# Sums of weights for a feed-forward layer on one Trainium2 core: smaller transfers and no pacing copies

## The chip, the core and the metric

The kernel runs on one core of one Trainium2 chip. A core has a matrix engine (TensorE; PE in the profile, with PEld for its weight loads), VectorE (DVE), ScalarE (ACT), GpSimd (POOL) and SyncE (SP), each with its own queue of instructions, and 16 DMA engines that all queues share. The metric is the device time of one execution in microseconds (us), and the median of several runs. A profile of one execution goes with it; times within it count from the start of its span.

## The reference, cut to what matters

One decoder layer on 512 tokens of width 1024 in float32: half a step of a gated feed-forward, an attention mixer with two branches, half a step of a second feed-forward, a last normalisation. The change touches the first feed-forward only.

```python
def _swiglu(x, w_gate, w_up, w_down):
    return (jax.nn.silu(x @ w_gate) * (x @ w_up)) @ w_down
...
h = h + FFN_HALF * _swiglu(_rmsnorm(h, norm_ffn1[i]), ffn1_gate[i], ffn1_up[i], ffn1_down[i])
```

`ffn1_gate` and `ffn1_up` are 1024 x 2816, `ffn1_down` is 2816 x 1024.

## The kernel before

**Numbers in two parts.** Every matrix product is made of three: each float32 operand is split into a high part that TensorE takes exactly and a low part, and high x high, high x low and low x high are added in PSUM. Weights come from DRAM as blocks of 512 KB (`raw`, four buffers, loaded by SP, line 137). ScalarE casts the high part (`whi`, line 145), VectorE subtracts for the low part (`wlo`, line 149), TensorE multiplies (`mm`, line 379, or line 747 in the units below). Blocks are split two ahead of their use. A block of the first feed-forward feeds 24 matmuls of 512 columns.

**The first feed-forward** (`ffn`, line 772) goes over 22 column tiles of 128 (f-tiles) in thirds: 0 to 7, 8 to 15, 16 to 21. After each third its part of `ffn1_down` is multiplied, in eight blocks, and added to `h` (line 821). In the first third, sums and differences of the activations are also made (`sums_of_u`), which the second third needs.

**The second third** is computed with seven half-size products instead of eight (`unit`, line 718), two f-tiles a unit, four units in all. Four of the seven multiply sums and differences of quarters of `ffn1_gate` and `ffn1_up`: s1 = u0 + u1, s3 = g0 + u0, s2 = s1 + g0, s4 = s2 + g1, where g0, g1, u0, u1 are the upper and lower halves of the two matrices in these columns. DMA makes these sums from DRAM to DRAM: GpSimd issues a plain copy (line 440) or an adding transfer (line 438) for each step of `unit_sums` (line 429). Each step that reads what an earlier one wrote waits for it in GpSimd's queue, and everything behind it in that queue waits too. SP loads the finished sums like other weights (`raw<-s`).

**The order of the sums.** `CHUNK` (line 32) says how many f-tiles one set of sums covers: 4, so there are two sets ("chunks") of 8 steps, each step a transfer of 512 rows of 2 KB. `adds` is the generator of these steps. Two steps are issued after the first f-tile that the loop computes (f == 3 at that place). Each further step goes through `pace` (line 713): GpSimd first copies one column of something just computed (`G`, or `h` in the down product), so that the step can't be issued before that exists. After the loops what is left of the steps is issued.

**What else stands in GpSimd's queue** at that time: the masks of the attention (`build_masks`, lines 538 to 552), issued from `side_work` (line 927) after the fourth f-tile; the last of them clears `fold`. One f-tile later VectorE writes into `fold` (lines 931 and 932) and so waits for GpSimd. Later `rope_tables` (line 554) has ScalarE issue two loads of 31 integers each into `pc` (line 562), one integer to a partition, and VectorE reads `pc` at line 565, between the low parts of the down blocks.

Of the kernel before, what the change touches and what calls it, by code (L numbers as in the profile page):

```python
# [8 lines left out]
F32 = mybir.dt.float32  # L9
# [19 lines left out]
NEVER = 1e9  # L29
STEPS = (1, 0), (5, 0), (2, 0), (1, 1), (5, 1), (2, 1), (6, 0), (6, 1), (3, 0), (3, 1), (4, 0), (4, 1), (7, 0), (7, 1)  # L30
PRODUCTS = 1, 6, 5, 2, 7, 3, 4
CHUNK = 4
LAST_ROWS = 0, 1, 4, 5, 2, 3
LAST_ORDER = 0, 1, 4, 5, 2, 3
TOP = 3e38
# [23 lines left out]
def f32(ap):  # L59
    return ap.bitcast(F32)  # L60


class Weights:
# [110 lines left out]
    def next(self):  # L174
        i = self.pos
        self.prep(i + self.AHEAD)
        self.pos += 1
        return self.place(i)
# [178 lines left out]
def layer(ctx, tc, a, out):  # L357
    nc = tc.nc
    tensor, scalar, vector, gpsimd = nc.tensor, nc.scalar, nc.vector, nc.gpsimd
    const = ctx.enter_context(tc.tile_pool(name="const", bufs=1))  # L360
# [7 lines left out]
    def acc(filler=True):  # L368
        turn[0] += 1
        return psum.tile([128, 512], F32, name="acc" if filler else ("acc", "o", "s")[turn[0] % 3])  # L370
# [48 lines left out]
    def chunks(tiles):  # L419
        return [(f, min(CHUNK, tiles[1] - f)) for f in range(tiles[0], tiles[1], CHUNK)]  # L420

# [3 lines left out]
    def sum_tile(n, f, k):  # L425
        t, i = s_sums[n, f, k]
        return t if i == 0 else s_sums[n, t, k][0]

    def unit_sums(n):


        for f, nf in chunks(UNITS[n]):
            g0, g1, u0, u1 = (half(n, what, kh, f, nf) for what in ("gate", "up") for kh in range(2))
            s1, s2, s3, s4 = (sum_tile(n, f, k) for k in range(1, 5))
            for o, i, add in ((s1, u0, 0), (s3, g0, 0), (s1, u1, 1), (s3, u0, 1), (s2, s1, 0), (s2, g0, 1), (s4, s2, 0),
                              (s4, g1, 1)):
                if add:
                    gpsimd.dma_start(o, i, accum_op=OP.add)
                else:
                    gpsimd.dma_start(o, i)  # L440
                yield

    def unit_block(n, f, m):
# [4 lines left out]
        k = {5: 1, 6: 2, 7: 3, 3: 4}[m]  # L448
        c = (f - UNITS[n][0]) % CHUNK * 128
        return sum_tile(n, f, k).rearrange("(k p) c -> p k c", p=128)[:, :, c:c + 256]  # L450
# [59 lines left out]
    G = main.tile([128, 16, S], F32R, name="G")  # L510
# [122 lines left out]
    def col_of(sums):  # L633
        v = temp.tile([128, 4], F32, name="nv", bufs=1)
        vector.tensor_scalar(v, sums, 1.0 / D, EPS, op0=OP.mult, op1=OP.add)
        y = temp.tile([128, 4], F32, name="ny", bufs=1)
        gpsimd.tensor_tensor(y, v, mhalf, op=OP.pow)
        b = temp.tile([128, 4], F32, name="nb", bufs=1)
        vector.tensor_tensor(b, y, y, op=OP.mult)
        vector.tensor_tensor(b, b, v, op=OP.mult)  # L640
        vector.tensor_scalar(b, b, -0.5, 1.5, op0=OP.mult, op1=OP.add)
        col = temp.tile([128, 4], F32, name="rcol", bufs=1)
        vector.tensor_tensor(col, y, b, op=OP.mult)
        return col

    def norm_rows(col):
        dg = sqacc.rearrange("p (t c) -> p t c", t=4)
        for t in range(4):
            vector.tensor_scalar(dg[:, t], ident, col[:, t:t + 1], None, op0=OP.mult)
        ps = tbank()  # L650
        for t in range(4):
            mm(ps[:, t], ones, dg[:, t], True, True)
        scalar.copy(r_b, flat(ps))


    def mm3(ps, w, x, n, amid=None):
        (wh, wl), (xh, xl) = w, x
        for k in range(n):
            if amid is not None and k == n * 3 // 4:
                amid()  # L660
            mm(ps, wh[:, k], xh(k), k == 0, False)
            mm(ps, wh[:, k], xl(k), False, False)
            mm(ps, wl[:, k], xh(k), False, k == n - 1)
# [4 lines left out]
    def swiglu(pg, pu, j):  # L668
        z = temp.tile([128, S], F32, name="z")
        vector.tensor_tensor(z, pg, r_b, op=OP.mult)  # L670
        s = temp.tile([128, S], F32, name="s")
        scalar.activation(s, z, AF.Silu)
        t = temp.tile([128, S], F32, name="t")
        vector.tensor_tensor(t, pu, r_b, op=OP.mult)
        g = temp.tile([128, S], F32, name="g")
        vector.tensor_tensor(g, s, t, op=OP.mult)
        split(G[:, j], G[:, 8 + j], g)
# [3 lines left out]
    def sums_of_u(n, k):  # L681


        g1, g2 = gains[:, n, k:k + 1], gains[:, n, 4 + k:5 + k]
        (h11, h12), (h21, h22) = ((h[:, d, :256], h[:, d, 256:]) for d in (k, 4 + k))
        b, p, q = (temp.tile([128, 2, 256], F32, name=name) for name in "zst")
        scalar.activation(b[:, 0], h12, AF.Identity, scale=g1)
        scalar.activation(b[:, 1], h22, AF.Identity, scale=g2)
        vector.scalar_tensor_tensor(p[:, 0], h11, g1, b[:, 0], op0=OP.mult, op1=OP.subtract)
        vector.tensor_tensor(p[:, 1], b[:, 1], p[:, 0], op=OP.add)  # L690
        vector.tensor_tensor(q[:, 0], b[:, 0], b[:, 1], op=OP.subtract)
        vector.scalar_tensor_tensor(q[:, 1], h21, g2, p[:, 1], op0=OP.mult, op1=OP.subtract)
        for i, x in ((0, p), (2, q)):
            split(both["hi"][:, k, i:i + 2], both["lo"][:, k, i:i + 2], x)
# [11 lines left out]
    def settle(todo):  # L706
        for x in todo:
            x()
        todo.clear()

    pace_t = const.tile([128, 1], F32, name="pace")

    def pace(adds, after):

        gpsimd.tensor_copy(pace_t, after)
        next(adds, None)

    def unit(j):


# [51 lines left out]
    def ffn(after, begun, side, sums, early):  # L772


        norm = {}

        def col():
            norm["col"] = col_of(sums)

        def rows():  # L780
            norm_rows(norm["col"])
            for j, b in enumerate(begun):
                swiglu(*b, j)

        lo, hi = UNITS[1]
        adds = unit_sums(1)
        for third, (f0, f1) in enumerate(THIRDS):
            f = f0 + (len(begun) if f0 == 0 else 0)
            while f < f1:
                if lo <= f < hi:  # L790
                    unit(f - f0)
                    f += 2
                    if f > lo + 2:
                        next(early, None)
                    continue
                first = f == len(begun)
                pg = acc(False)
                mm3(pg, W.next(), u_in, KD, col if first else None)
                pu = acc(False)
                mm3(pu, W.next(), u_in, KD, rows if first else None)  # L800
                swiglu(pg, pu, f - f0)
                f += 1
                if third == 0:
                    if f > 4:
                        sums_of_u(0, f - 5)
                    if f == 3:
                        next(adds)
                        next(adds)
                    for j in (8 + f - 1, f - 1) if f < 7 else (f - 1,):
                        pace(adds, f32(G[:, j, :1]))  # L810
                else:
                    next(early, None)
                next(side, None)
            settle(later)
            settle(owed)
            for d in range(KD):
                po = acc(False)
                mm3(po, W.next(), g_in, f1 - f0)
                if third == 2 and d < KD - 1:
                    W.prep(W.pos + W.AHEAD)  # L820
                vector.scalar_tensor_tensor(h[:, d], po, 0.5, h[:, d], op0=OP.mult, op1=OP.add)
                if third == 0:
                    next(side, None)
                    if d < 4:
                        pace(adds, h[:, d, :1])
                if third == 1 and d in (0, 2, 4, 6, 7):
                    next(early, None)
                if third == 2:
                    after(d)
        for g in (adds, side, early):  # L830
            for _ in g:
                pass
# [4 lines left out]
    with pool("h1") as h_pool, pool("temp1", 2) as temp, pool("tables") as tables, ExitStack() as starting:  # L837
        start = starting.enter_context(pool("start"))
        h = h_pool.tile([128, KD, S], F32, name="h")
# [107 lines left out]
        with pool("stage", 2) as stage, pool("both") as sums_pool:  # L947
            both["hi"], both["lo"] = (sums_pool.tile([128, 4, 4, 256], F32R, name=n) for n in ("bhi", "blo"))
            ffn(to_mix, begun, side_work(), sums=sums0, early=W.early(stage))
# [3 lines left out]
    with ExitStack() as mixing:  # L953
# [703 lines left out]
        h = h_pool.tile([128, KD, S], F32, name="h")  # L1657
# [247 lines left out]
```

## Time and profile before

| What | Before |
|---|---|
| median of 3 runs | 1129.09 us (1125.06 to 1131.6) |
| the profiled execution, its own time | 1128.45 us |
| its span | 1126.7 us |
| mean granted clock of TensorE | 0.994 |
| bytes moved by DMA | 186.28 MB, mean 165 GB/s |
| q0 (transfers that GpSimd issues) | 10880 packets, 33.56 MB, 12.8% of 16 engines |
| q1 (transfers that SP issues) | 190536 packets, 147.38 MB, 43.2% of 16 engines |
| first issue of a sum, last issue of a sum | 35.16 us, 142.09 us |

The profiled execution is one of many; its span runs from the first to the last instruction, and its own time is 1.75 us longer. The first third of the feed-forward with its down product reaches to about 153 us, the four units from there to about 231 us. Rows of the chain and of an engine's instructions begin with their start and length in microseconds; in brackets stands how long the engine had been idle and what ended that. Rows of waits give the total, the times and the longest.

### The profile page before, as it was taken

The numbers are of one execution on the slowest core, as the hardware profiler recorded it, in microseconds if no ns is written. First come the engines' busy times: TensorE is split into PE (matmuls) and PEld (weight loads), VectorE is DVE, ScalarE is ACT, GpSimd is POOL, SyncE is SP. The second block draws the span as 40 slices with busy tenths as digits, with TensorE's granted clock in tenths as the row PEclk, the third lists the DMA queues.
The fourth block names the chain that finished last, engine by engine and source line by source line (L and its number), as shares of the span: only waits on it lengthen the run. The fifth ranks groups of instructions, "written<-read, shape, count | busy, mean of one in ns | idle before, by whom it ended". The sixth has DMA issues, their size and how long they took to land.

```text
span 1126.7 us, 15645 instructions
## 1 busy us (share of the span) xinstructions
PE 1104.6 (98%) x5859; PEld 946.4 (84%) x5859; DVE 714.4 (63%) x1299; ACT 495.7 (44%) x922; POOL 184.0 (16%) x219
## 2 busy tenths in 40 slices
PE   9999899999999999999999999999999999999997
PEld 8878699988888999989888888888888888888876
DVE  5667468874566569887777646654567754685553
ACT  5435134542334446766667643433334332342332
POOL 0122000000001235654333422120000000000002
PEclk9999899999999999999999999999999999999999
DMA  7499966698766446737667455633234633354212
GB/s 230 150 250 266 250 179 195 203 297 267 225 205 196 130 121 172 187 118 179 203 163 235 117 178 165 177 94 112 76 99 144 191 89 113 103 176 132 83 68 75
DMA packets 204164, 186.28 MB, mean 165 GB/s; under 512 B 6772, under 2 KB 175544, under 8 KB 203960
## 3 DMA queue, kind: packets, MB, share of 16 engines
q1 hardware_dynamic: 190536, 147.38, 43.2%
q0 software_dynamic: 10880, 33.56, 12.8%
q10 hardware_dynamic: 2672, 4.35, 1.0%
q8 instruction: 46, 0.75, 0.3%
q14 instruction: 30, 0.25, 0.1%
HBM read 165.34 MB, written 53.48 MB: 194 GB/s over the span
## 4 chain that ended last, share of the span: by engine, by line
PE 89%; DVE 4%; issue 2%; DMA 2%; ACT 2%; POOL 1%; POOLq 0%; ACTq 0%; DVEq 0%; SPq 0%
PE acc L379 32%; PE s L379 23%; PE o L379 23%; PE o L747 3%; PE tp L1596 2%; PE s L747 2%; PE acc L747 2%; DMA pc<-in_positions_dram 1%; DVE wlo L149 1%; ACT whi L145 1%; DMA raw<-in_cmp_k_w_dram 1%; PE tp L379 1%; DVE turn_a L1294 0%; PE tp L885 0%; PE tp L1222 0%
## 5 line engine op out<-in xcount | busy, mean ns | idle before, releaser
L149 DVE TENSOR_TENSOR wlo<-raw,whi 128x1024 fp32r<-128x1024 f32 (+2 forms) x201 | 229.9, 1166 | 44.7 <-ACT whi L145 44.4
L145 ACT CAST whi<-raw 128x1024 fp32r<-128x1024 f32 (+2 forms) x226 | 203.0, 925 | 110.0 <-PE acc L379 30.5
L379 PE MATMUL acc<-uh,whi 128*128 128x512 f32 x296 | 117.9, 398 | 0.0
L379 PE MATMUL acc<-uh,wlo 128*128 128x512 f32 x296 | 115.8, 391 | 0.0
L379 PE MATMUL acc<-ul,whi 128*128 128x512 f32 x296 | 115.6, 390 | 0.0
L379 PE MATMUL o<-uh,wlo 128*128 128x512 f32 x208 | 81.2, 391 | 1.3 <-DVE wlo L149 1.3
L379 PE MATMUL o<-uh,whi 128*128 128x512 f32 x208 | 82.2, 395 | 0.0
L379 PE MATMUL o<-ul,whi 128*128 128x512 f32 x208 | 81.2, 390 | 0.0
L379 PE MATMUL s<-uh,whi 128*128 128x512 f32 x200 | 78.0, 390 | 0.0
L379 PE MATMUL s<-uh,wlo 128*128 128x512 f32 x200 | 77.9, 390 | 0.0
L379 PE MATMUL s<-ul,whi 128*128 128x512 f32 x200 | 77.9, 390 | 0.0
L379 PE MATMUL acc<-whi,uh 128*128 128x256 f32 x224 | 66.1, 295 | 1.3 <-ACT whi L145 1.3
L379 PEld LDWEIGHTS acc<-uh,wlo 128*128 128x128 f32 x296 | 55.6, 188 | 12.3 <-DVE wlo L149 0.4
L379 PEld LDWEIGHTS acc<-ul,whi 128*128 128x128 f32 x296 | 55.7, 188 | 10.4
L379 PEld LDWEIGHTS acc<-uh,whi 128*128 128x128 f32 x296 | 55.7, 188 | 10.3
L379 PE MATMUL acc<-wlo,uh 128*128 128x256 f32 x224 | 63.7, 284 | 0.1
L379 PE MATMUL acc<-whi,ul 128*128 128x256 f32 x224 | 63.6, 284 | 0.0
L1831 POOL TENSOR_TENSOR o_t<-o_t,g_b 128x512 f32<-128x512 f32 (+1 forms) x5 | 5.9, 1184 | 335.0 <-ACT z L1825 335.0
L1611 DVE TENSOR_TENSOR pts<-tp,pts 128x512 fp32r<-128x512 f32 (+1 forms) x62 | 41.8, 687 | 21.3 <-ACT pts L1608 20.7
L379 PE MATMUL s<-G,whi 128*128 128x512 f32 x160 | 51.4, 404 | 0.0
L1510 ACT ACTIVATE pbuf<-s,m 128x256 f32<-128x256 f32 (+3 forms) x96 | 47.5, 503 | 8.0 <-DVE c L1520 4.2
L379 PE MATMUL acc<-G,whi 128*128 128x512 f32 x164 | 50.5, 390 | 0.0
(403 smaller groups left out, 2645.2 us busy)
## 6 DMA issues: line engine op xcount, KB each, us to landing
raw<-in_ffn_gate_dram SPq DMA_DIRECT2D x42, 512.0 KB, 3.9
raw<-in_ffn_up_dram SPq DMA_DIRECT2D x38, 512.0 KB, 5.4
raw<-in_ffn_down_dram SPq DMA_DIRECT2D x34, 512.0 KB, 4.5
t<-in_ffn_down_dram POOLq DMA_DIRECT2D x12, 1024.0 KB, 9.5
raw<-in_w_in_dram SPq DMA_DIRECT2D x20, 512.0 KB, 5.2
raw<-s SPq DMA_DIRECT2D x16, 512.0 KB, 4.5
raw<-t SPq DMA_DIRECT2D x16, 512.0 KB, 3.8
s<-in_ffn_up_dram POOLq DMA_DIRECT2D x6, 1024.0 KB, 12.3
```

The source lines that it names most:

```text
L145: self.nc.scalar.copy(self.place(i)[0][:, k0:k1], self.raw[i][:, k0:k1])
L149: engine.tensor_tensor(lo, self.raw[i][:, k0:k1], f32(hi), op=OP.subtract)
L379: tensor.matmul(out, lhsT, rhs, start=start, stop=stop)
L747: tensor.matmul(o, a_[:, n], x(k), start=new and n == step == 0, stop=n == 7 and step == 2, skip_group_check=True)
L1510: scalar.activation(u.p[:, hd], b.view[:, j], AF.Exp, bias=u.m[:, hd:hd + 1], scale=-1.0, accum_out=u.sum[:, hd:hd + 1])
L1596: tensor.transpose(ps[:w, hd], u.p[:, hd, kb * w:kb * w + w], ident)
L1611: vector.tensor_tensor(p.lo, flat(b.ps)[:w], f32(p.hi), op=OP.subtract)
L1831: gpsimd.tensor_tensor(y, y, g_b[:, cs], op=OP.mult)
```

## The change

`CHUNK` goes from 4 to 2: four chunks of 8 steps, each step a transfer of 512 rows of 1 KB, 0.5 MB instead of 1 MB. The bytes summed are the same. `pace` and its one-column copies are gone. Instead, up to six steps are issued after each f-tile of the first third.

```diff
-CHUNK = 4
+CHUNK = 2
...
-    pace_t = const.tile([128, 1], F32, name="pace")
-
-    def pace(adds, after):
-
-        gpsimd.tensor_copy(pace_t, after)
-        next(adds, None)
-
...
                 if third == 0:
                     if f > 4:
                         sums_of_u(0, f - 5)
-                    if f == 3:
-                        next(adds)
-                        next(adds)
-                    for j in (8 + f - 1, f - 1) if f < 7 else (f - 1,):
-                        pace(adds, f32(G[:, j, :1]))
+                    for _ in range(6):
+                        next(adds, None)
...
                 if third == 0:
                     next(side, None)
-                    if d < 4:
-                        pace(adds, h[:, d, :1])
```

**First place: GpSimd, from the first step of the sums to the masks.** In a name such as `s_8_1_84`, 8 is the f-tile with which the chunk begins, 1 is the sum (s1 to s4), and the last number is a running one; in brackets stand the semaphores waited for, `DMASW` those of GpSimd's transfers. Before:

```order
L440 DMA s_8_1_84<-in_ffn_up_dram 512x512
L440 DMA s_8_3_86<-in_ffn_gate_dram 512x512
L715 COPY pace<-G 128x1 [waits DVE_49]
L438 DMA s_8_1_84<-in_ffn_up_dram 512x512 [waits DMASW0_49]
L715 COPY pace<-G 128x1 [waits Activation_49,Pool_49]
L438 DMA s_8_3_86<-in_ffn_up_dram 512x512 [waits DMASW1_49]
L715 COPY pace<-G 128x1 [waits DVE_49,Pool_49]
L440 DMA s_8_2_85<-s_8_1_84 16x16384 [waits DMASW2_49]
L715 COPY pace<-G 128x1 [waits Activation_49,Pool_49]
L438 DMA s_8_2_85<-in_ffn_gate_dram 512x512 [waits DMASW4_49]
L539 MEMSET mask_n 128x512
```

The same stretch now, without its first row (the first step, a plain load of s1, as before):

```order
L440 DMA s_8_3_86<-in_ffn_gate_dram 512x256
L438 DMA s_8_1_84<-in_ffn_up_dram 512x256 [waits DMASW0_49]
L438 DMA s_8_3_86<-in_ffn_up_dram 512x256 [waits DMASW1_49]
L440 DMA s_8_2_85<-s_8_1_84 16x8192 [waits DMASW2_49]
L438 DMA s_8_2_85<-in_ffn_gate_dram 512x256 [waits DMASW4_49]
L440 DMA s_8_4_87<-s_8_2_85 16x8192 [waits DMASW5_49]
L438 DMA s_8_4_87<-in_ffn_gate_dram 512x256 [waits DMASW6_49]
L440 DMA s_10_1_88<-in_ffn_up_dram 512x256
L440 DMA s_10_3_90<-in_ffn_gate_dram 512x256
L438 DMA s_10_1_88<-in_ffn_up_dram 512x256 [waits DMASW0_49]
L438 DMA s_10_3_90<-in_ffn_up_dram 512x256 [waits DMASW3_49,DMASW1_49]
L539 MEMSET mask_n 128x512
```

The masks stood behind six steps of the first chunk and their paces; now they stand behind twelve steps, the whole first chunk and the first four of the second.

**Second place: SP, the loads of the second unit** (the sums among its seven blocks; `DMAHW` are semaphores of SP's own transfers). Before:

```order
L137 DMA raw<-s_8_2_85 128x4x256 [waits DMAHW4_49,DVE_49]
L137 DMA raw<-s_8_1_84 128x4x256 [waits DMAHW5_49,DVE_49]
L137 DMA raw<-in_ffn_gate_dram 128x4x256 [waits DMAHW6_49,DVE_49]
L137 DMA raw<-s_8_3_86 128x4x256 [waits DMAHW7_49,DVE_49]
L137 DMA raw<-s_8_4_87 128x4x256 [waits DMAHW0_49,DVE_49]
```

Now:

```order
L137 DMA raw<-s_10_2_89 128x4x256 [waits DMAHW4_49,DMASW5_49,DVE_49]
L137 DMA raw<-s_10_1_88 128x4x256 [waits DMAHW5_49,DMASW2_49,DVE_49]
L137 DMA raw<-in_ffn_gate_dram 128x4x256 [waits DMAHW6_49,DVE_49]
L137 DMA raw<-s_10_3_90 128x4x256 [waits DMAHW7_49,DMASW3_49,DVE_49]
L137 DMA raw<-s_10_4_91 128x4x256 [waits DMAHW0_49,DMASW7_49,DVE_49]
```

The loads stand where they stood; each of the four sums now waits for a transfer of its own chunk, where before the first unit had already waited for the chunk that both share. The fourth unit gets the same four waits. On TensorE, VectorE and ScalarE the order of instructions is unchanged.

## The prediction, made before the changed kernel was run

> **What bounds the kernel now.** I read the page first, then who waits for whom, then the chain that ended last, and last the queues. The page's busy times:
>
> ```profile
> PE 1104.6 (98%) x5859; PEld 946.4 (84%) x5859; DVE 714.4 (63%) x1299; ACT 495.7 (44%) x922; POOL 184.0 (16%) x219
> ```
>
> TensorE is busy for 98% of the span: a change that leaves its work alone can gain only from its 22 us of idle time and from slow clock, but can lose without limit. The waits that ended TensorE's idle time (total, times, longest):
>
> ```profile
> PE s L379 <- DVE wlo L149: 5.4, 1, 5.4
> PE o L379 <- DVE wlo L149: 1.8, 2, 1.3
> ```
>
> Both waits are for the low part of a weight block, which VectorE makes. The chain of waits shows where (start, length, what):
>
> ```profile
> 73.12 1.01 POOL s L438
> ...
> 77.23 0.21 POOL fold L552
> ...
> 79.17 5.32 PE o L379 x22
> ...
> 100.88 5.08 PE s L379 x22
> ...
> 109.18 12.12 DMA pc<-in_positions_dram
> ...
> 123.13 8.19 PE s L379 x22
> ```
>
> Place A: GpSimd issues an adding transfer at 73.1, then builds the masks up to `fold`, and only then can VectorE write into `fold` and turn to the weights. Place B: VectorE waits 12.12 us for `pc`, two loads of 31 integers each, with the low parts of the next weights behind it in its queue. Busy times in the stretch behind B (length; PE, PEld, DVE, ACT, POOL busy; granted clock; DMA share; GB/s):
>
> ```profile
> 125.00:130.00 5.00, 5.00 (x14) 3.91 (x13) 4.49 (x10) 1.05 (x1) 1.19 (x2) 0.56 0.75 142
> ```
>
> B costs 5.4 us of waiting, and then the clock falls to 0.56: 22 matmuls take 8.19 us that took 5.08 us at 100.88. **B is 5.4 + 3.1 = 8.5 us, A is 1.3 us.** That is the whole prize, 9.8 us.
>
> **Why B happens.** The DMA queues in two stretches, 114 to 118 and then 126 to 135 (packets, MB, share of 16 engines); q0 carries GpSimd's sums, q1 the weights, q10 the loads that ScalarE issued, `pc` among them:
>
> ```profile
> q0 software_dynamic: 332, 0.67, 89.5%
> q1 hardware_dynamic: 334, 0.17, 21.2%
> q10 hardware_dynamic: 20, 0.00, 0.3%
> ```
>
> ```profile
> q0 software_dynamic: 528, 1.05, 70.4%
> ```
>
> The rows of the sums and the packets of the weights go one for one, 332 to 334, although a row of 2 KB takes 4 x 16 x 0.895 / 332 = 172 ns and a packet of weights 4 x 16 x 0.212 / 334 = 41 ns. The 20 packets of q10 come one in 200 ns, about a row and a weight packet: I read that as one DMA engine giving each queue a turn, with all of `pc` on that engine. Its 62 integers at 0.2 us are 12.4 us, which is the wait seen. So the length of a row sets the wait.
>
> **What the change costs, A.** GpSimd's instructions now (start, length):
>
> ```profile
> 35.16 0.90 POOL L440 DMA_DIRECT2D s<-in_ffn_up_dram  x1
> 36.06 0.66 POOL L440 DMA_DIRECT2D s<-in_ffn_gate_dram  x1
> 54.26 0.19 POOL L715 COPY pace<-G 128x1 f32<-128x1 f32 x1 [17.54 <-DVE G L383]
> ...
> 73.10 1.04 POOL L438 DMA_DIRECT2D s<-in_ffn_gate_dram  x1 [8.38 <-DMA s<-s]
> ...
> 84.70 0.56 POOL L440 DMA_DIRECT2D s<-s  x1 [7.14 <-DMA s<-in_ffn_gate_dram]
> ...
> 90.60 1.05 POOL L438 DMA_DIRECT2D s<-in_ffn_gate_dram  x1 [5.15 <-DMA s<-s]
> ...
> 125.50 1.01 POOL L438 DMA_DIRECT2D s<-in_ffn_gate_dram  x1 [1.51 <-DMA s<-s]
> ...
> 135.48 0.52 POOL L440 DMA_DIRECT2D s<-s  x1 [7.98 <-DMA s<-in_ffn_gate_dram]
> ```
>
> Before the masks stand 6 transfers of 1 MB and their paces, the first of which holds the queue for 17.5 us. After the change 12 transfers of 0.5 MB stand there and no pace. Price of one, from its issue to the issue that waited for it: an add of 1 MB 135.48 - 125.50 = 9.98 us, of which data is 9 us x 70.4% = 6.3 us and the rest, 3.65 us, I keep as fixed; a copy `s<-s` 90.60 - 84.70 = 5.9 us. The queue from 85 to 90, and from 37 to 45, when the first two loads ran:
>
> ```profile
> q0 software_dynamic: 32, 1.05, 62.6%
> ```
>
> ```profile
> q0 software_dynamic: 544, 2.10, 72.5%
> ```
>
> The copy's data is 5 x 62.6% = 3.1 us, fixed 2.8 us; a first load's is 8 x 72.5% / 2 = 2.9 us. Halving the data alone: add 3.65 + 3.15 = 6.8, copy 2.8 + 1.55 = 4.4, first load 3.65 + 1.45 = 5.1 us.
>
> The chain then runs: first load issued at 35.16; first add at 40.3; copy 47.1; add 51.5; copy 58.3; last add of the first chunk 62.7, landed 69.5; the two first loads of the second chunk queue behind it, 71.0 and 72.4; at 72.4 the second add after them is issued, and the masks follow. From such an issue to the end of `fold` takes 77.44 - 73.10 = 4.3 us: 76.7. Weight packets between the rows add some 1 us: **77.7, against 77.4 now.** VectorE needs 79.17 - 77.44 = 1.7 us more before TensorE runs, so A grows by 0.3 us: what the paces gave back is eaten by more steps.
>
> Bounds: TensorE would not wait at all with `fold` ready by 79.17 - 1.3 - 1.7 = 76.2. If the fixed parts halve too, it is ready at 66.5, and A's 1.3 us go. If a half transfer takes as long as a whole one now, the same chain gives 41.7, 51.7, 57.6, 67.6, 73.5, 83.5, 89.3, and 93.6 for `fold`: +16.2 us. I take the middle because a weight packet of 512 bytes costs 41 ns and a row four times as long 172 ns: time goes nearly with bytes.
>
> The rule of the Trainium skill that speaks against this change is in DMA: Bandwidth & Descriptors, Bandwidth: batch transfers to 1 MiB or more. Its section on the anatomy of one DMA gives 2.0 us plus the bytes over 436 GB/s, so 4.4 us for 1 MB and 3.2 us for 0.5 MB, 73%. My prices are 68% for the add and 75% for the copy. With 73% on both, the three adds of the chain take 0.5 us more each, and the estimate would be some 1.4 us later than the sum below; the add measured here, 9.98 us, is 2.3 times that page's figure.
>
> **B.** Going on at the same prices, with those 1 us: an add issued at 72, behind it a second one; copy 79; add 83.5; copy 90.3; add 94.7; first loads of the third chunk landed at 103.0 and 104.4. Then come its two adds, with data from about 106 to 113. `pc` is still asked for at 109, so it still meets adds. But a turn is now 86 + 28 = 114 ns instead of 200 ns: at most 12.12 x 114 / 200 = 6.9 us; at least some 2.0 us, the quickest small load here:
>
> ```profile
> w<-in_cmp_v_w_dram SPq DMA_DIRECT2D x1, 64.0 KB, 2.0
> ```
>
> Asked for at 109.2 + 0.3, it lands between 111.5 and 116.4. From its landing, 109.18 + 12.12 = 121.30, to TensorE's start at 123.13 are 1.8 us, so TensorE could go on at 118.2 at the latest; it needs that at 123.13 - 5.4 + 0.3 = 118.0. By the halved turn the stall is 0 to 0.2 us, and all 5.4 us if the turn doesn't shrink. I keep 1.0 us, near the first, without a slow clock: after the 1.3 us at A, 22 matmuls took 5.32 us.
>
> **The rest.** The removed paces free no bound engine: GpSimd is 16% busy. The 32 issues instead of 16, at about 1 us, are GpSimd's own time, within waits that are counted above. The sums end later than now: some 31 us a chunk, 35 + 4 x 31 + 7 = 166. They are read by SP's loads, the first pair of the first unit and of the last:
>
> ```profile
> 129.66 4.79 SPq L137 DMA_DIRECT2D raw<-s  x2
> ...
> 201.01 3.25 SPq L137 DMA_DIRECT2D raw<-s  x2
> ```
>
> The fourth chunk is first read at 201, so the eight new waits on SP's queue (second place above) are met 35 us ahead, and I price them at nothing; without that cover SP's later loads would queue behind the waiting one and TensorE after them. From 142 to 166 the sums also run beside the loads of the units, four raw buffers deep: nothing, with up to 3 us in the range.
>
> **Sum**, against the profiled execution's own 1128.45 us (span 1126.7; the median shown, 1129.09, is 0.06% above, and I don't shift for it): 1128.45 + 0.3 - 8.5 + 1.0 = **1121.3 us**.
>
> **Rivals.**
> 1. Slower: the masks come too late. One mechanism, the chain ahead of `fold` on GpSimd; if transfers cost per piece and not per byte, `fold` comes at 93.6, +16.2 us, and with B gone 1128.45 + 16.2 - 8.5 = 1136.2, with B kept 1144.7. It eats the gain from `fold` at 84.9 on, and is slower by 0.5% from 90.5 on. For it: three adds and two copies in series, all with fixed parts I only inferred. Against: 41 ns against 172 ns. 15%.
> 2. No gain: `pc` still waits 12 us, since the sums are never idle without paces, or the paces were not what delayed them. Of GpSimd's waiting, 27.5 us was for paces, the rest for transfers:
>
> ```profile
> POOL pace L715 <- DVE G L383: 20.1, 2, 17.5
> POOL pace L715 <- DVE h L821: 7.4, 2, 6.6
> ```
>
> B stays: 1128.8 us. 23%.
> 3. Both stalls go: `pc` falls between bursts and `fold` is there by 76.2: 1128.45 - 9.8 = 1118.7 us. 17%.
> 4. The forecast, 1119.5 to 1124.5: 45%.
>
> **Numbers.** About 0.5% is what a measurement can tell here. Faster by more: rival 3 and four fifths of the forecast, 53%; within 0.5%: rival 2 and the rest, 32%; slower: 15%. The range: down to both stalls gone with 2 us of scatter, 1116.5, up to 1131.5, which leaves out most of rival 1 and little else.
>
> **What would show it.** Right: the `pace` rows gone, GpSimd's mask rows starting near 73 and `fold` ending at 75 to 80; rows of the sums at about half of 172 ns; VectorE's wait for `pc` at most 7 us; TensorE's 5.4 us wait and the clock below 1 near 125 gone. Wrong: `fold` after 85 with TensorE waiting there as long; a row of 1 KB that takes as long as one of 2 KB; a new TensorE wait after 150 for `raw<-s`.

## The result, and the profile after

| | before | changed |
|---|---|---|
| median of 8 runs each | 1128.46 us (1125.06 to 1132.91) | 1121.93 us (1118.47 to 1125.61) |
| ratio | | 0.9944, 95% interval 0.992 to 0.9968 |
| profiled execution: time, span | 1128.45, 1126.7 us | 1118.47, 1116.8 us |

The change gained 6.5 us of the median. The profiled execution of the changed kernel is the fastest of its eight runs. The changed kernel's profile, in the views shown before: first TensorE's waits (total, times, longest).

```profile
PE o L379 <- DVE wlo L149: 3.0, 2, 2.5
```

The 5.4 us wait of place B is gone; the wait of place A went from 1.3 to 2.5 us. The chain of waits has the rest (start, length, what):

```profile
78.07 0.21 POOL fold L552
...
80.01 6.64 PE o L379 x22
86.65 5.44 PE s L379 x24
...
114.01 5.44 PE o L379 x24
119.45 5.44 PE s L379 x24
...
146.65 2.87 PE acc L740 x24
```

At A the 22 matmuls behind the wait now take 6.64 us, where they took 5.32: the clock drops here, as it did at B before. At B, near 119, block follows block without a gap. The first unit starts at 146.65, and in the profile before, in the same view, here:

```profile
153.09 2.87 PE acc L747 x24
```

That is 6.4 us earlier. Busy times of the changed kernel at A and at B (length; PE, PEld, DVE, ACT, POOL; granted clock; DMA share; GB/s):

```profile
80.00:84.00 4.00, 3.99 (x12) 3.22 (x13) 3.15 (x5) 1.46 (x3) 0.58 (x1) 0.63 1.05 301
...
115.00:120.00 5.00, 5.00 (x24) 4.14 (x23) 3.72 (x11) 0.69 (x1) 1.00 (x1) 1.00 0.51 165
```

The span fell by 9.9 us in these two executions, 3.5 us of it behind the changed part: the first store of `zd`, in the attention, comes 8.8 us earlier (528.6 to 519.8), the last matmul 10.0. The largest piece lies near 488. There TensorE waits 1.8 us for `pbuf` in both kernels, and only in the profile before is the clock halved behind that wait, which costs 1.5 us. Busy times in that stretch, before and changed, in the columns used above:

```profile
485.00:490.00 5.00, 3.68 (x24) 3.36 (x25) 4.66 (x21) 3.98 (x18) 3.04 (x4) 0.78 0.00 0
```

```profile
477.00:482.00 5.00, 3.23 (x29) 2.74 (x28) 4.69 (x18) 3.33 (x14) 3.04 (x4) 1.00 0.00 0
```

Of the kernels below, the profiled executions of e1 and e7 have that slow stretch too, those of e3 and e8 don't; and e7's profiled execution has a mean granted clock of 0.997, two others of the same kernel 0.999. So the stretch seems to come and go between executions, and it isn't counted as the change's. The other 2 us come in small steps from 380 on and stay unexplained. What the change did is the 6.4 us at the first unit, and the medians differ by 6.5. GpSimd and VectorE of the changed kernel, and last VectorE's row in the kernel before:

```profile
34.83 0.90 POOL L440 DMA_DIRECT2D s<-in_ffn_up_dram  x1
...
40.42 1.09 POOL L438 DMA_DIRECT2D s<-in_ffn_up_dram  x1 [4.03 <-DMA s<-in_ffn_up_dram]
...
46.92 0.52 POOL L440 DMA_DIRECT2D s<-s  x1 [4.03 <-DMA s<-in_ffn_up_dram]
51.78 1.04 POOL L438 DMA_DIRECT2D s<-in_ffn_gate_dram  x1 [4.33 <-DMA s<-s]
58.12 0.52 POOL L440 DMA_DIRECT2D s<-s  x1 [5.31 <-DMA s<-in_ffn_gate_dram]
63.40 1.01 POOL L438 DMA_DIRECT2D s<-in_ffn_gate_dram  x1 [4.76 <-DMA s<-s]
...
73.93 1.05 POOL L438 DMA_DIRECT2D s<-in_ffn_up_dram  x1 [0.34 <-issue]
...
78.01 0.26 POOL L552 MEMSET fold<- 128x192 f32 x1
```

```profile
116.07 0.15 DVE L565 CAST p<-pc 128x1 f32<-128x1 int32 x1 [4.98 <-DMA pc<-in_positions_dram]
```

```profile
121.42 0.15 DVE L565 CAST p<-pc 128x1 f32<-128x1 int32 x1 [12.49 <-DMA pc<-in_positions_dram]
```

The twelve transfers run without a pace and still fill the time to 73.9; `fold` is ready at 78.3. VectorE waits 5.0 us for `pc` instead of 12.5 us.

### The profile page after: what moved, and what is told of

The parts are those of the page before. It is cut to its first block, busy times and chain, and to the rows that moved or that the text cites. A ratio compares the mean times of both kernels' runs of the same rounds, so it can differ in the third digit from the quotient of the medians.

```text
span 1116.8 us, 15632 instructions
## 1 busy us (share of the span) xinstructions
PE 1098.8 (98%) x5859; PEld 942.0 (84%) x5859; DVE 717.8 (64%) x1299; ACT 495.8 (44%) x922; POOL 193.3 (17%) x221
## 4 chain that ended last, share of the span: by engine, by line
PE 90%; DVE 4%; DMA 3%; issue 2%; ACT 1%; POOL 1%; POOLq 0%; DVEq 0%; ACTq 0%; SPq 0%
PE acc L379 32%; PE o L379 24%; PE s L379 23%; PE o L740 3%; PE tp L1584 2%; PE s L740 2%; PE acc L740 2%; DMA s<-in_ffn_up_dram 1%; DVE wlo L149 1%; DMA s<-s 1%; DMA s<-in_ffn_gate_dram 1%; DMA raw<-in_cmp_k_w_dram 1%; DVE turn_a L1282 0%; PE tp L379 0%; PE tp L1210 0%
## 5 line engine op out<-in xcount | busy, mean ns | idle before, releaser
L379 PE MATMUL acc<-ul,whi 128*128 128x512 f32 x296 | 115.5, 390 | 0.0
```

The source lines that it names most:

```text
L379: tensor.matmul(out, lhsT, rhs, start=start, stop=stop)
```

## The experiments

Two questions. Are A and B all there is? And which part of the change took B away: the shorter rows, or the missing paces? The rival to the theory of short turns is that only the moment decides, that is, what happens to stand in the DMA queues when `pc` is asked for.

In the table "first unit" is the start of the first matmul of the first unit, the measure of what happens in this part. Waits and starts are those of one profiled execution each; a time with (1) behind it is a single execution. In all these executions GpSimd's small `ny` step, from which the sums start, stands between 33.9 and 34.7.

| kernel | rows | paces | masks | TensorE waits at A, B | VectorE waits for `pc` | first unit | time (runs) |
|---|---|---|---|---|---|---|---|
| before | 2 KB | yes | after 6 transfers | 1.3, 5.4 | 12.5 | 152.9 | 1128.46 (8) |
| changed | 1 KB | no | after 12 | 2.5, 0 | 5.0 | 146.5 | 1121.93 (8) |
| e1 | 1 KB | no | first | 0, 0 | 5.5 | 142.7 | 1115.43 (4) |
| e2 | 2 KB | yes | first | 0, 10.1 | 17.2 | 155.4 | 1130.76 (1) |
| e3 | 2 KB | no | first | 0, 0.4 | 7.5 | 143.0 | 1115.64 (1) |
| e4 | 1 KB | yes | first | 0, 1.5 | 8.6 | 144.4 | 1119.98 (1) |
| e5 | 2 KB | no | after 12 | 18.6, 0 | 3.4 | 164.3 | 1138.37 (1) |
| e9, before with `pc` cut | 2 KB | yes | after 6 | 1.5, 0 | 6.4 | 144.5 | 1119.07 (4) |
| e7, before with masks first, `pc` at the start | 2 KB | yes | first | 0, 0 | none | 142.6 | 1115.82 (4) |
| e8, changed with the same | 1 KB | no | first | 0, 0 | none | 142.8 | 1115.02 (6) |

**e1: the changed kernel, masks first.** GpSimd is idle until 34; the masks go there.

```diff
         W.load(2)
         load_rest()
+        build_masks()
...
             yield
-            build_masks()
             yield
```

> The changed kernel with the masks issued on GpSimd ahead of the first sum, in the time in which it waits for the first norm. Theory (A is only the masks standing behind twelve transfers): VectorE's wait for fold (6.2 us) and TensorE's wait at A (2.5 us) go, and with them the half clock behind it (22 matmuls in 6.64 us instead of 5.32): the first unit starts 3.8 us earlier, near 142.9 instead of 146.65, and the time is 3.8 us under the changed kernel's 1121.9, near 1118. pc is asked near 107 and still lands in time, since the adds of the third chunk end near 112. Rival (the weights behind fold would be late anyway, by their own transfers): TensorE still waits 2 us or more near 78, for a low part whose raw block came late, and nothing is gained.

Measured: ratio to before 0.9876 (0.9854 to 0.9897), 1115.43 us. In its chain of waits the blocks at A and behind run on:

```profile
77.44 5.44 PE o L379 x24
82.88 5.44 PE s L379 x24
```

The theory holds: the first unit starts 3.8 us earlier, as expected. The time fell by more than that, 6.5 us against the changed kernel's median, of which I can explain 3.8. The two profiled executions differ by 2.1 us only, since e1's has the half clock in the attention, which cost 1.5 us above, and the changed kernel's has not. The four runs of e1 lie within 1.5 us, the eight of the changed kernel within 7.1 us. That fits a wait at A that differs between executions; e10 below has one more such wait.

**e2: the kernel before, masks first.** The same move, in the kernel before.

> The kernel before (rows of 2 KB, paces) with the masks first. Theory: A's 1.3 us go, B stays whole, since neither its rows nor its timing change: VectorE waits 11 to 13 us for pc, TensorE 5 to 6 us, the clock halves again; the first unit starts near 151.8. Rival (B hangs on how the masks delay the sums): the wait for pc falls below 8 us.

Neither: A went, and B grew. TensorE's and VectorE's waits:

```profile
PE s L379 <- DVE wlo L149: 10.1, 1, 10.1
```

```profile
DVE p L565 <- DMA pc<-in_positions_dram: 17.2, 1, 17.2
```

`pc` is asked for 1.3 us earlier, at 107.9, and lands later, at 124.7. In this kernel's queues from 113 to 120:

```profile
q0 software_dynamic: 589, 1.17, 90.2%
q1 hardware_dynamic: 590, 0.30, 21.4%
q10 hardware_dynamic: 36, 0.00, 0.3%
```

One for one again, and 36 integers in 7 us, 0.19 us each. The turns are as before; now 49 of the last 64 packets of q10 fall before 121.5, beside the adds, and the other 15 come at 123.8, behind the copy `s<-s`. Taking a wait away made the next one dearer by 4.7 us: this one execution took 1130.76 us, no less than before.

**e3: rows of 2 KB, no paces, masks first** (`CHUNK = 4` in e1).

> Rows of 2 KB without paces, masks first: of the two parts of the change only the removed paces. Theory of the turns (each of the 62 integers waits for one row): at the prices of whole transfers the second chunk's third step, a single add, has its data from 110 to 117, so pc, asked near 107, gets turns of 0.2 us and waits 8 to 11 us; TensorE waits 1 to 4 us at B; the first unit starts near 145 to 148. Rival 1 (removing the paces was what cured B): pc waits under 5 us, TensorE not at all, unit start near 143. Rival 2 (the row length alone matters, not when adds run): pc waits 12 us and TensorE 5 us as before.

The wait for `pc` was 7.5 us, TensorE's 0.4 us, the first unit at 143.0: just under the low end of what the turns were to give, and for TensorE what rival 1 said. The sums' second chunk had no add until one was issued at 111.21; from 110.4 to 111.4 the queues moved 631 packets of weights and one of q0, and the last 32 packets of q10 came at 113.5, in 0.2 us. So `pc` met hardly a row, and long rows do no harm where they don't stand beside `pc`.

**e4: rows of 1 KB, paces kept, masks first.** The edit to the kernel before, beside the move of e1:

```diff
-CHUNK = 4
+CHUNK = 2
...
         gpsimd.tensor_copy(pace_t, after)
         next(adds, None)
+        next(adds, None)
...
-                        next(adds)
-                        next(adds)
+                        for _ in range(4):
+                            next(adds)
```

> Rows of 1 KB with the paces kept (two steps behind each pace, four ahead of the first), masks first: of the two parts of the change only the smaller rows. Theory of the turns: whatever adds stand beside pc, its wait is at most 7 us, TensorE doesn't wait at B, and the first unit starts near 143 to 144. Rival (the paces and their bunching of transfers made B): pc waits 9 us or more, TensorE 3 us or more, unit start 147 or later.

The wait for `pc` was 8.6 us, not at most 7, and TensorE waited 1.5 us. Its queues from 111.5 to 114.5 say why:

```profile
q0 software_dynamic: 275, 1.00, 81.3%
q1 hardware_dynamic: 412, 0.21, 23.2%
q10 hardware_dynamic: 16, 0.00, 0.3%
```

1.00 MB in 275 packets is 3.6 KB each. These are not adds but the first, plain loads of the third chunk (issued at 106.5 and 107.2), and those move in packets of some 4 KB whatever the row. The 16 packets of q10 came one in 0.19 us. So the expectation reckoned with adds and met loads; what `pc` waits beside adds of 1 KB this execution doesn't show.

That answers the second question as far as one execution each can: with the masks first, the kernel before has 10.1 us of B (e2), without paces 0.4 (e3), with short rows 1.5 (e4). Either half takes most of B away, and both do it by what stands beside `pc` when it moves. For the changed kernel itself the queues say the same, in the section on the prediction.

**e5: the changed kernel with rows of 2 KB** (`CHUNK = 4`, masks where the change leaves them).

> The changed kernel with rows of 2 KB again (two chunks, no paces, masks behind twelve transfers of 1 MB). Theory (the prediction's chain with prices of whole transfers): the twelfth issue comes near 93 to 98 instead of 73.9, fold near 97 to 102 instead of 78.3; TensorE waits 18 to 23 us at A and the clock halves for some us behind it; pc, asked 20 us later, costs at most 2 us; the first unit starts near 163 to 170, the time is 1134 to 1142, slower than before. Rival (the length of the transfers doesn't matter for the masks, only their number): fold near 78 as in the changed kernel, and a time near 1122.

Its waits of TensorE and VectorE:

```profile
PE o L379 <- DVE wlo L149: 18.6, 1, 18.6
```

```profile
DVE fold L919 <- POOL fold L552: 22.3, 1, 22.3
```

`fold` ended at 94.7, a little ahead of the 97 to 102 expected, TensorE waited 18.6 us, the time was 1138.37 us. So without paces it is the size of the transfers that holds the masks, and this half of the change alone, the missing paces, was slower in its one execution. The other half alone, short rows with paces and the masks in their old place, was not run.

**e9: the kernel before, `pc` loaded in other pieces.** Nothing of the sums is touched.

```diff
         for g in range(2):
-            nc.scalar.dma_start(pc[g * 32:g * 32 + 31], dram(a["positions"], 31, [[16, 31], [1, 1]]))
+            for i, n in ((0, 30), (30, 1)):
+                nc.scalar.dma_start(pc[g * 32 + i:g * 32 + i + n],
+                                    dram(a["positions"], 31 + 16 * i, [[16, n], [1, 1]]))
```

> The kernel before, each load of 31 integers into pc cut into one of 30 partitions and one of 1; nothing else. Theory (31 can't be dealt to several DMA engines, so all integers stand in one engine's queue and each lets a row of the sums go ahead): 30 integers go to 15 engines, each lets two or three rows ahead; VectorE's wait for pc falls from 12.5 to 3 to 6 us, TensorE's 5.4 us at B and the half clock go, the first unit starts near 144.6 and the time falls by 8 us, ratio 0.993. Rival (any small load takes 12 us in such a burst, since the queue of the weights starves, or the raw weights are late anyway): wait for pc 9 us or more, TensorE waits 3 us or more, ratio 0.997 or above.

Ratio 0.9907 (0.9884 to 0.9929), a larger gain than the 0.993 expected. VectorE's waits:

```profile
DVE p L567 <- DMA pc<-in_positions_dram: 6.4, 1, 6.4
```

6.4 us, a little more than expected, and TensorE didn't wait at B; the first unit starts at 144.5. The same integers, the same rows beside them, and the adds where they were: what was slow is 31 integers standing in one engine's queue. ScalarE still waited 12.7 us for a raw block, which TensorE never felt, so the weights were not the rival they looked like.

**e7: the kernel before with both waits taken away by order.** Masks first, and the two loads of `pc` moved from `rope_tables` to the start, on SP behind `load_rest`.

> The kernel before (rows of 2 KB, paces) with both waits taken away by order alone: masks on GpSimd ahead of the sums, pc loaded at the start. Theory (the change's whole effect is these two waits, and smaller transfers and missing paces are worth nothing beside them): no TensorE wait above 1 us between 40 and 230, first unit near 143, time 9.8 us under before and equal to the changed kernel with masks first (ratio to before 0.985 to 0.991). Rival (the bursts of 1 MB transfers delay the weights too): with pc out of the way ScalarE waits for a raw block of the down weights at 110 to 125 and TensorE waits 2 us or more there; ratio 0.991 to 0.997.

Ratio 0.9882 (0.9863 to 0.9902), the first unit at 142.6, no TensorE wait above 0.4 us there. Large transfers and paces cost nothing more that shows here.

**e8: the changed kernel with the same two moves.**

> The changed kernel with masks first and pc loaded at the start. Theory (two waits are all there is to gain in this part): equal to the changed kernel with masks first and to the kernel before with both moves, 1115 to 1116.5, first unit near 143. Rival (pc's wait of 5.5 us still cost something there, or the smaller transfers help the weights): 1 us or more under both.

1115.02 us, ratio 0.9883 (0.9863 to 0.9903): no different from e7 or e1. Each of the three is faster than both kernels of this case; e7 does it without the change.

**e10: the changed kernel with `pc` asked for at 72.** The loads move into `side_work`, ahead of VectorE's write into `fold`.

> The changed kernel with pc asked for at 72, beside the second chunk's two adds (74 to 81), when no weights are loaded: a look at how fast its 62 integers go between rows of 1 KB. Theory of the turns: one integer per row of 1 KB, 0.10 to 0.13 us each, against 0.20 us beside rows of 2 KB, so 45 to 62 of the ScalarE queue's packets of 4 bytes fall between 74.5 and 80.5. Rival (a turn has a fixed length whatever the row): 0.2 us each, about 30 packets in that time. TensorE doesn't wait at B, A is unchanged, the first unit starts near 146.7 as in the changed kernel.

Inconclusive for the turns: `pc` had landed near 74 and the adds were issued at 75.7 and 77.1. But the chain of the twelve transfers ran 3 us later than in the changed kernel's own profile:

```profile
81.22 0.21 POOL fold L552
...
83.16 7.23 PE o L379 x22
```

TensorE waited 5.3 us at A, and the time was 1122.60 us. The loads of `pc` aren't what began that: the first chunk's last add was issued at 64.57, 1.2 us later than in the changed kernel, and `pc` was asked for only at 72.5. From that add to the next one it took 11.2 us here, 9.1 us in the changed kernel, and 9.6 us in e11 below with sixteen such loads. So the chain ahead of `fold`, and A with it, differs by some us between executions.

**e11 and e12: the turn, measured.** In `side_work`, eight times the two loads, so that they lie beside adds in any case; in the changed kernel and in the kernel before.

```diff
...
+            more = [tables.tile([128, 1], I32, name="more%d" % i) for i in range(7)]
+            for i in range(8):
+                for g in range(2):
+                    nc.scalar.dma_start((more[i] if i < 7 else pc)[g * 32:g * 32 + 31],
+                                        dram(a["positions"], 31, [[16, 31], [1, 1]]))
```

> A measurement of the turn: the changed kernel with the loads of 31 integers into pc asked for at 72 and repeated eight times, so that they lie beside the second chunk's adds whatever the phase; the repeats go to tiles that nothing reads. Theory of the turns: while rows of 1 KB run and no weights, the ScalarE queue's 4-byte packets come one per 0.10 to 0.13 us. Rival (fixed turn): one per 0.2 us. ScalarE spends some 5 us on the issues, so A grows by a few us and the time means nothing here.

> The same measurement in the kernel before, beside its add of rows of 2 KB from 77 to 84. Theory of the turns: one 4-byte packet per 0.18 to 0.21 us while that add runs without weights. Rival (fixed turn): the same rate as beside rows of 1 KB. The time means nothing here.

The queues of e11 from 77 to 79, with rows of 1 KB and no weights, then those of e12 from 80 to 82, with rows of 2 KB and no weights:

```profile
q0 software_dynamic: 386, 0.39, 121.4%
q10 hardware_dynamic: 23, 0.00, 1.7%
```

```profile
q0 software_dynamic: 206, 0.42, 114.5%
q10 hardware_dynamic: 12, 0.00, 0.9%
```

One engine's share of the rows is 386 / 16 = 24 and 206 / 16 = 13; the small packets are 23 and 12. So it is one for one in both, at 87 ns and 167 ns, each a little under the range expected. A turn is nearly as long as the row that stands in it, and half the row is about half the turn.

## Why the prediction was right, point by point

- **What bounds: right.** The prize was put at 9.8 us, and e1, e7 and e8, in which A and B are both gone, start the first unit 10.1 to 10.4 us earlier than before. All else in this part was worth no more than some half a microsecond.
- **The chain ahead of `fold`: right to 1.5 us, in part because errors cancel.** Forecast issues 40.3, 47.1, 51.5, 58.3, 62.7, 72.4; measured 40.4, 46.9, 51.8, 58.1, 63.4, 73.9, from a first issue 0.3 us earlier. The adds took 6.3 to 6.5 us where I had 6.8, the copies 4.9 and 5.3 us where I had 4.4. That prices go with bytes and fixed parts stay was the right middle: a row of 1 KB took 2 us x 16 x 1.214 / 386 = 101 ns in e11, one of 2 KB 178 ns in e12.
- **A: mis-sized.** The term "A grows by 0.3 us" measured 2.5 us: `fold` came 0.6 us later than forecast, TensorE waited 1.2 us longer than before, and the clock, which I had left alone, halved behind a wait of 2.5 us, 6.64 - 5.32 = 1.3 us.
- **B: right in size, short of its mechanism.** I kept 1.0 us of 8.5 and nothing was left. The wait, 5.0 us, lies within the 2.0 to 6.9 forecast. But the shorter turn isn't what ended it. The changed kernel's queues from 111.9 to 114.2 and from 114.2 to 115.5:

```profile
q0 software_dynamic: 337, 0.33, 90.7%
q1 hardware_dynamic: 333, 0.17, 25.0%
q10 hardware_dynamic: 62, 0.01, 3.9%
```

```profile
q0 software_dynamic: 23, 0.44, 88.9%
q1 hardware_dynamic: 652, 0.33, 84.1%
q10 hardware_dynamic: 64, 0.00, 2.8%
```

The 62 packets beside the adds, 0.01 MB, are rows of `inv`, the load that ScalarE issues ahead of `pc` (line 558). The 64 later ones, `pc`'s 62 integers among them, went in 1.3 us, 20 ns each, once the adds were over; in the kernel before the adds lasted until past 120. The half-length adds were through sooner. e3 shows the same with whole rows: with the masks first, either half of the change alone leaves 0.4 or 1.5 us of B.
- **The 12.4 us read into B: right in total by luck.** I took 62 integers at 0.2 us for the whole wait of 12.12 us. ScalarE's queue in the kernel before, from 109 to 112.6, from there to 120.1, and on to 121:

```profile
q10 hardware_dynamic: 144, 0.02, 5.9%
...
q10 hardware_dynamic: 38, 0.00, 0.3%
...
q10 hardware_dynamic: 26, 0.00, 1.6%
```

The first 144 packets, 0.02 MB, are `inv`'s. Then 38 came in 7.5 us, 0.2 us each, and once the adds were over 26 in 0.9 us. So the turn is as I read it, but turns made some 7.5 us of the wait, and over 3 us passed before the first integer moved, in the changed kernel too (asked for at 111.0, the first after 114.2).
- **The sum.** The terms measured are 2.5 - 8.5 = -6.0 us, against -7.2 forecast; with the 0.3 us by which the first issue came earlier that is, to 0.1 us, the 6.4 us at the first unit. The medians' difference is -6.5 us. A was 2.2 us dearer than forecast and B 1.0 us cheaper, so the two misses partly cancel, and that much of the closeness is luck.
- **The rest at nothing: right.** The fourth chunk's last add was issued at 169.8, 4 us behind my estimate for its end but 25 us ahead of its first reader, at 194.6, and no TensorE wait above 0.4 us appeared in the units.
- **Rival 1 (masks too late)** is real, and e5 is it: 18.6 us with transfers of 1 MB. The halved transfers kept it away, not the missing paces. **Rival 2** (B stays) fell. **Rival 3** (both stalls go) needed `fold` by 76.2 and got it at 78.3; e1 is where it comes true.

## What to carry to other kernels

Where a wait ends on a tiny load, look at how its shape is dealt over the DMA engines and at what moves beside it: here cutting 31 into 30 + 1 was worth 0.93% by itself, more than the change. Before a queue is filled with long waiting transfers, put the short work that others need ahead of them. And take waits away together with what they shield: removing A alone made B grow from 5.4 to 10.1 us (e2, one execution).

## What the runs showed of the hardware

- An adding transfer's row costs about as much as a plain packet of twice its size: 178 ns for 2 KB (e12), against 8 us x 16 x 0.725 / 544 = 171 ns for the first loads' packets, 2.10 MB in 544, about 4 KB each.
- The plain first loads merge short rows into packets of some 4 KB (e4), so a smaller row doesn't shorten the turns beside them.
- TensorE's clock halved behind waits of 2.5 and 5.4 us, not behind 1.3 us (5.32 us for 22 matmuls). Behind the same wait of 1.8 us it halved in the profiled execution before and not in the changed one, so the length of the wait alone doesn't decide.
